# One integer step of a top-k selection, and the low parts of some matmul weights, moved from VectorE to GpSimd

## The chip, the cores and the metric

The kernel runs on one core of one Trainium2 chip. The metric is the device time of one execution in microseconds (us). The engines are named as in the profile: PE is TensorE's matmuls, PEld its weight loads, DVE is VectorE, ACT is ScalarE, POOL is GpSimd, SP is SyncE, whose queue issues most DMAs. Each engine runs its own queue in order; an instruction that waits for another engine holds back all that stand behind it.

## What is computed

Two layers of a decoder trunk on 1024 tokens of width 1024, fp32 throughout. Each layer is one wide projection, a sparse attention (branch A), a gated delta rule (branch B) and an output projection:

```
for layer in range(DEPTH):                      # 2
    h = rms_norm(x, norm_gain[layer])
    (q_a, k_a, v_a, z_a, q_i, k_i, w_i, qkv_b, z_b, beta_l, a_l, gate_l) = split(h @ w_in[layer])
    y_a = dsa_attention(rope(q_a), rope(k_a), v_a, rope(q_i), rope(rms_norm(k_i)), w_i) * silu(z_a)
    y_b = rms_norm(gated_delta_rule(silu(conv(qkv_b)), ...)) * silu(z_b)
    x = x + (sigmoid(gA) * y_a + sigmoid(gB) * y_b) @ w_out[layer]

# in dsa_attention, for each block of 128 queries
iscore = einsum('bqhs,bqh->bqs', relu(einsum('bqhd,bsd->bqhs', qib, k_idx)), wb)
iscore = where(causal, iscore, -inf)
_, sel = lax.top_k(iscore, 256)                 # each query attends to its 256 best keys
```

The change touches how the 256 best keys are found and how the weights of the first gates (`sigmoid(gA) * silu(z_a)`) are prepared.

## The kernel before, in words

A matmul in full fp32 is made of three in a rounded format: the operand is split into a high part and the rest (`split`, L152 to L156). ACT writes the high part by a cast (`w_hi`, L155), DVE subtracts it from the raw weight (`w_lo`, L156). A product is then hi·hi, hi·lo and lo·hi. `w_tiles` holds three raw tiles (`w_raw`, loaded by SP's queue) and eight of each part, so a raw tile is free for the next load when both parts are made.

In each layer `token_phase` (L411) runs the projections for q, k and v of branch A in three chunks of eight token blocks. For each block ACT copies the result to a `stage` tile (L426), POOL turns it by the rotary tables (`rope`, L270 to L275, two-input operations) and POOL's queue stores it (`qs` L432, `ks` L434, `vs` L435). After them come four gates of branch A (`gate_a`, `GATES[0]` = 4): each projects two pairs of weight tiles over two halves of the tokens. ACT takes a tanh of each result (`th`, L700) and frees its PSUM bank (tags `acc` and `wide` in turn); DVE joins it (`gate<-th,acc` and `gate<-th,gate`, L701), where the first of the two still reads the bank `acc`.

Beside the projections runs the selection (`self.beside`, taken a little further by `tick` after some matmuls). For the six blocks of 128 queries that have more than 256 keys it finds the 256th largest score of each query by bisecting the bits of its float, from bit 30 down to bit 0. There are two groups, `([5], [4, 3, 2])` and `([7], [6])`, interleaved: in each group DVE counts the keys above the threshold for the first list (L603) and ACT for the second (`t_sign`, L621, a sign with accumulation). A half-step then forms on DVE the candidate for the next bit (`cand`, L625), compares the counts (`dec`, L627) and sets the bits (`bits`, L628). The signs of the group's next half-step wait for these bits. Behind the 31 steps a tail on DVE (L632 to L686) corrects the thresholds and breaks ties with a scan per block (L675 to L685); ACT makes the signs (L665) in two buffers `t_sign`, so the sign of a block waits for the maximum (L682) of the block two before it.

`feature_phase` follows (branch B, tags `more` and `acc`): its first matmuls are those of `kf`. Its two tiles `xp` are cleared at four columns by DVE (L725). They lie where the `stage` tiles lay, so this memset waits until the last `ks` store has read its `stage`. The bank `more` is one that a gate's `wide` used.

A scheduler sets the order in each engine's queue: the program is laid out by priorities (`high_priority`, `issue_after`), and what it takes for an operation's cost moves the rows that follow.

Of the kernel before, what the change touches and what calls it, by code (L numbers as in the profile page):

```python
# [25 lines left out]
F32 = mybir.dt.float32  # L26
# [3 lines left out]
I32 = mybir.dt.int32  # L30
AF = mybir.ActivationFunctionType
OP = mybir.AluOpType
# [4 lines left out]
P = 128  # L37
# [64 lines left out]
class Trunk:  # L102
# [47 lines left out]
            nc.vector.scalar_tensor_tensor(y, t, 1.5, y, op0=OP.add, op1=OP.mult)  # L150
        return y

    def split(self, hi, lo, src):

        self.nc.scalar.copy(hi, src)  # L155
        self.nc.vector.tensor_sub(lo, src, hi.bitcast(F32))  # L156


    def identity(self):
# [6 lines left out]
    def constants(self, first):  # L166
        nc, c = self.nc, self.const
        self.ones = c.tile([P, P], F32, name="ones")
        nc.gpsimd.memset(self.ones, 1.0)

        def tri(name, fill_in, fill_out, cm, step, base, dtype=F32):
            m = c.tile([P, P], dtype, name=name)
            nc.gpsimd.memset(m, fill_in)
            nc.gpsimd.affine_select(m, m, pattern=[[step, P]], compare_op=OP.is_ge, fill=fill_out, base=base,
                                    channel_multiplier=cm)
            return m


        self.tri_in = tri("tri_in", 1.0, 0.0, -1, 1, 0)
        self.tri_out = tri("tri_out", 1.0, 0.0, 1, -1, -1)  # L180
        self.tri_mid = c.tile([P, P], F32, name="tri_mid")
        nc.vector.tensor_copy(self.tri_mid[64:], self.tri_in[64:])
        nc.vector.tensor_scalar(self.tri_mid[:64], self.tri_out[:64], -1.0, None, op0=OP.mult)
        self.causal_sel = tri("causal_sel", BIG, -BIG, 1, -1, 0)
        self.causal01 = c.tile([P, 2 * P], BF16, name="causal01")
        nc.gpsimd.memset(self.causal01, 0.0)
        nc.gpsimd.affine_select(self.causal01[:, P:], self.causal01[:, P:], pattern=[[-1, P]],
                                compare_op=OP.is_ge, fill=MASKED, base=0, channel_multiplier=1)

        self.xinit = c.tile([P, 8, 32], F32, name="xinit")  # L190
        nc.gpsimd.memset(self.xinit, 0.0)
        for q in range(4):
            nc.gpsimd.affine_select(self.xinit[32 * q:32 * q + 32], self.xinit[32 * q:32 * q + 32],
                                    pattern=[[4, 8], [-1, 32]], compare_op=OP.not_equal, fill=1.0, base=q,
                                    channel_multiplier=0)
        self.rope_tables()

        self.feat, self.ig, self.nexpa, self.dtb = [], [], [], []
        for l in range(self.depth):
            rows = first.tile([P, P], F32, name="rows", bufs=2)  # L200
            nc.sync.dma_start(out=rows[0:96], in_=self.conv_w[l].rearrange("j (t c) -> (j t) c", c=P))
            nc.sync.dma_start(out=rows[96:97], in_=self.gdn_gain[l][None, :])
            pt = self.tr()
            nc.tensor.transpose(pt[:, :97], rows[:97], self.ident[:97, :97])
            f = c.tile([P, 97], F32, name=f"feat{l}")
            nc.vector.tensor_copy(f, pt[:, :97])
            nc.vector.tensor_scalar(f[:, 96:97], f[:, 96:97], 0.25, None, op0=OP.mult)
            self.feat.append(f)
            g = c.tile([P, IDXD], F32, name=f"ig{l}")
            nc.sync.dma_start(out=g, in_=ap(self.idx_gain[l], 0, [[0, P], [1, IDXD]]))  # L210
            self.ig.append(g)
            al = c.tile([P, 8], F32, name=f"al{l}")
            nc.sync.dma_start(out=al, in_=ap(self.a_log[l], 0, [[0, P], [1, 8]]))
            nc.scalar.activation(al, al, AF.Exp)
            nc.vector.tensor_scalar(al, al, -1.0, None, op0=OP.mult)
            self.nexpa.append(al)
            db = c.tile([P, 8], F32, name=f"db{l}")
            nc.sync.dma_start(out=db, in_=ap(self.dt_bias[l], 0, [[0, P], [1, 8]]))
            self.dtb.append(db)
# [113 lines left out]
    def w_tiles(self, srcs, n):  # L333

        nc, pool = self.nc, self.wp
        raw = pool.tile([P, 512], F32, name="w_raw", bufs=3)
        for o, w, a in srcs:
            dst = raw[:, o:o + w]
            if len(a.shape) == 3:
                dst = dst.rearrange("p (k c) -> p k c", k=a.shape[1])  # L340
            nc.sync.dma_start(out=dst, in_=a)
        hi = pool.tile([P, 512], F32R, name="w_hi", bufs=KT)
        lo = pool.tile([P, 512], F32R, name="w_lo", bufs=KT)
        self.split(hi[:, :n], lo[:, :n], raw[:, :n])
        return hi, lo

    def token_weights(self, w, pieces, now=True):
# [64 lines left out]
    def token_phase(self, l, ip, ht, first):  # L412
        nc, tc = self.nc, self.tc
# [7 lines left out]
        raw = ip.tile([P, T, IDXW], F32, name="idx_raw")  # L421
        copy = lambda t, a, o: nc.scalar.copy(raw[:, t, o:o + 300], a)

        def evac(t, a, chunk):
            st = ip.tile([P, 512], F32, name="stage", bufs=3)
            nc.scalar.copy(st, a)  # L426
            rows = slice(t * P, (t + 1) * P)
            heads = 4 if chunk < 2 else 2
            v = st[:, :heads * P].rearrange("p (o h d) -> p o h d", o=1, d=P)
            self.rope(ip, v, slice(t, t + 1), self.rope_a, heads, nc.gpsimd)  # L430
            if chunk < 2:
                nc.gpsimd.dma_start(out=self.qs[rows, chunk * 512:chunk * 512 + 512], in_=st)  # L432
            else:
                nc.gpsimd.dma_start(out=self.ks[rows], in_=st[:, :256])  # L434
                nc.gpsimd.dma_start(out=self.vs[rows], in_=st[:, 256:])  # L435
# [11 lines left out]
        with tc.tile_pool(name="sel", bufs=1) as p, self.banks(wide=(2, 2)), ExitStack() as scoring:  # L447
            ps = scoring.enter_context(tc.tile_pool(name="tok", bufs=1))
            scores = {t: p.tile([P, (t + 1) * P], F32, name=f"scores{t}") for t in SEL}
            select = interleave([self.select(p, i, scores, *st) for i, st in enumerate(SEL_STAGES)])  # L450
            self.beside = itertools.chain(self.index_scores(l, ps, raw, scores), closing(scoring), select)

            for ch in range(3):
                self.proj_tokens(qkv[ch], ht, lambda t, a: evac(t, a, ch), then=qkv[ch + 1] if ch < 2 else None)
            for f in range(GATES[0]):
                self.gate_a(l, ht, f, itertools.cycle(("acc", "wide")))
            for _ in self.beside or ():
                pass
            self.beside = None
# [125 lines left out]
    def select(self, p, which, scores, on_dve, on_act):  # L585
# [6 lines left out]
        nc = self.nc  # L592
        blocks, n_dve = on_dve + on_act, len(on_dve)
        nb = len(blocks)
        sc = [scores[t] for t in blocks]
        mk = lambda n, dt=F32: p.tile([P, 4], dt, name=f"{n}{which}")[:, :nb]
        cnt, tau, dec = mk("t_cnt"), mk("t_tau"), mk("t_dec", I32)
        bits, cand, neg, neg1 = mk("t_bits", I32), mk("t_cand", I32), mk("t_neg", I32), mk("t_neg1", I32)
        f = lambda a, i: a[:, i:i + 1].bitcast(F32)

        def count(i, thr, op):
# [4 lines left out]
        for i in range(nb):  # L606
            count(i, 0.0, OP.is_ge)
            n = sc[i].shape[1]
            nc.vector.memset(tau[:, i:i + 1], float(n - TOPK if i < n_dve else n - 2 * TOPK))
        nc.vector.tensor_scalar(neg, cnt, float(TOPK), None, op0=OP.is_lt)  # L610
        nc.vector.tensor_scalar(neg1, neg, 2.0, 1.0, op0=OP.mult, op1=OP.add)
        nc.vector.tensor_scalar(bits, neg, 31, None, op0=OP.logical_shift_left)
        nc.vector.tensor_scalar(bits, bits, 1 << 30, None, op0=OP.bitwise_or)  # L613
        yield SEL_COST


        for b in range(30, -1, -1):
            for i in range(n_dve, nb):
                n = sc[i].shape[1]
                junk = p.tile([P, S], F16, name="t_sign", bufs=2)  # L620
                nc.scalar.activation(junk[:, :n], sc[i], AF.Sign, bias=f(bits, i), scale=-1.0,  # L621
                                     accum_out=cnt[:, i:i + 1])
            for i in range(n_dve):
                count(i, f(bits, i), OP.is_lt)
            nc.vector.scalar_tensor_tensor(cand, neg1 if b else neg, max(b - 1, 0), bits, op0=OP.logical_shift_left,  # L625
                                           op1=OP.bitwise_xor)
            nc.vector.tensor_tensor(dec, cnt, tau, op=OP.is_gt)  # L627
            nc.vector.scalar_tensor_tensor(bits, dec, b, cand, op0=OP.logical_shift_left, op1=OP.bitwise_xor)  # L628
            yield SEL_COST

        lo, far = mk("t_lo", I32), mk("t_far", I32)
# [36 lines left out]
        for i, t in enumerate(blocks):  # L668
            n = (t + 1) * P
# [536 lines left out]

    def run(self):
        nc, tc = self.nc, self.tc
        src = self.x.rearrange("b s d -> (b s) d")
        rest = None  # L1210
        for l in range(self.depth):
# [93 lines left out]
```

## Time and profile before

| | us |
|---|---|
| median of three runs (2589.47 to 2591.08) | 2590.01 |
| the profiled execution | 2589.74 |
| its span | 2588.0 |
| what lies around the span | 1.74 |
| PE busy | 2530.8 |
| DVE busy | 1879.1 |
| ACT busy | 1335.6 |
| POOL busy | 169.1 |

The stretch that the change touches is that of the gates and the selection's end: about 253 to 357 us in the first layer and 1528 to 1631 us in the second. PE is the engine on which the work of the program stands in a row; a gap before one of its matmuls is time that the other engines cost.

### The profile page before, as it was taken

The page shows a single profiled execution, that of the slowest core. Times are in us where ns is not written, and L with a number is a line of the kernel's source. Part 1 is how long each engine was busy: PE and PEld are TensorE (multiplying, and loading weights), DVE is VectorE, ACT ScalarE, POOL GpSimd, SP SyncE. Part 2 cuts the span into 40 slices and gives each one's busy share as a digit, 9 for nine tenths or more (in the row PEclk, how much of TensorE's full clock was granted, in tenths as well). Part 3 has the DMA queues.
Part 4 walks back from the last instruction along what each step waited for, and adds up shares of the span by engine and source line. Part 5 has one row for each costly group of instructions (what it writes and reads, how often), then busy time and mean ns, then how long its engine had stood idle before and what let it go on. Part 6 is the DMA issues. An engine that isn't in the chain of part 4 may idle for free. (4 is left out here: it accounts for less than half of the span.)

```text
span 2588.0 us, 41984 instructions
## 1 busy us (share of the span) xinstructions
PE 2530.8 (98%) x14858; PEld 2096.6 (81%) x14858; DVE 1879.1 (73%) x5092; ACT 1335.6 (52%) x3067; POOL 169.1 (7%) x438
## 2 busy tenths in 40 slices
PE   7999999999999999999999999999999999999998
PEld 7777787888888888898897777778888888878986
DVE  7569997777787763787465789777777787637876
ACT  5449944344444432787244597344444444338862
POOL 0234000000000000000002330000000000000000
PEclk9999999999999999999999999999999999999999
DMA  4122243223333331431421223333223323323314
GB/s 127 53 68 85 71 111 76 70 53 70 68 73 70 76 93 55 151 93 42 160 68 50 78 66 89 82 77 74 59 63 74 68 69 74 101 82 125 93 47 166
DMA packets 295415, 211.35 MB, mean 82 GB/s; under 512 B 72290, under 2 KB 252356, under 8 KB 295204
## 3 DMA queue, kind: packets, MB, share of 16 engines
q1 hardware_dynamic: 288388, 186.57, 26.8%
q0 software_dynamic: 6816, 22.09, 3.4%
q8 instruction: 117, 1.92, 0.3%
q14 instruction: 94, 0.77, 0.1%
HBM read 162.19 MB, written 46.40 MB: 81 GB/s over the span
## 5 line engine op out<-in xcount | busy, mean ns | idle before, releaser
L400 PE MATMUL acc<-hi_t,w_hi 128*128 128x512 f32 x1112 | 453.0, 407 | 3.3 <-ACT w_hi L155 3.1
L400 PE MATMUL acc<-hi_t,w_lo 128*128 128x512 f32 x1112 | 449.0, 404 | 3.5 <-DVE w_lo L156 3.5
L400 PE MATMUL acc<-lo_t,w_hi 128*128 128x512 f32 x1112 | 451.8, 406 | 0.0
L155 ACT CAST w_hi<-w_raw 128x512 fp32r<-128x512 f32 (+1 forms) x336 | 200.1, 603 | 269.6 <-PE acc L400 129.1
L156 DVE TENSOR_TENSOR w_lo<-w_raw,w_hi 128x512 fp32r<-128x512 f32 (+1 forms) x336 | 223.0, 670 | 137.5 <-ACT w_hi L155 118.4
L376 PE MATMUL acc<-w_hi,hi_t 128*128 128x512 f32 (+1 forms) x768 | 287.4, 375 | 5.4 <-ACT stage L426 2.8
L376 PE MATMUL acc<-w_lo,hi_t 128*128 128x512 f32 (+1 forms) x768 | 283.3, 369 | 2.6 <-DVE w_lo L156 2.5
L376 PE MATMUL acc<-w_hi,lo_t 128*128 128x512 f32 (+1 forms) x768 | 282.5, 368 | 0.0
L400 PEld LDWEIGHTS acc<-hi_t,w_lo 128*128 128x128 f32 x1112 | 209.5, 188 | 47.3 <-DVE w_lo L156 6.1
L400 PEld LDWEIGHTS acc<-hi_t,w_hi 128*128 128x128 f32 x1112 | 209.4, 188 | 46.9 <-ACT w_hi L155 5.8
L400 PEld LDWEIGHTS acc<-lo_t,w_hi 128*128 128x128 f32 x1112 | 209.5, 188 | 39.1
L400 PE MATMUL more<-hi_t,w_hi 128*128 128x512 f32 x488 | 200.2, 410 | 5.2 <-ACT th L700 5.2
L621 ACT ACTIVATE t_sign<-scores,t_bits 128x640 f16<-128x640 f32 x248 | 195.9, 794 | 16.2 <-DVE t_bits L613 13.3
L400 PE MATMUL more<-lo_t,w_hi 128*128 128x512 f32 x488 | 199.7, 409 | 0.0
L400 PE MATMUL more<-hi_t,w_lo 128*128 128x512 f32 x488 | 198.2, 406 | 0.0
L376 PEld LDWEIGHTS acc<-w_hi,hi_t 128*128 128x128 f32 x768 | 145.0, 189 | 38.3 <-issue 7.6
L376 PEld LDWEIGHTS acc<-w_lo,hi_t 128*128 128x128 f32 x768 | 145.3, 189 | 26.1 <-DVE w_lo L156 4.8
L376 PEld LDWEIGHTS acc<-w_hi,lo_t 128*128 128x128 f32 x768 | 145.2, 189 | 23.5 <-issue 1.0
L603 DVE TENSOR_SCALAR_CACHE_REDUCE t_junk<-scores,t_bits 128x768 f16<-128x768 f32 x124 | 142.1, 1146 | 4.2
L577 DVE SCALAR_TENSOR_TENSOR scores<-relu,w_idx,scores 128x384 f32<-128x384 f32 (+5 forms) x84 | 81.0, 965 | 65.0 <-ACT relu L570 60.4
L997 DVE TENSOR_TENSOR xtmp<-wide,xc 128x60 f32<-128x60 f32 (+24 forms) x496 | 105.9, 213 | 14.2
L999 DVE TENSOR_TENSOR xc<-xc,xtmp 128x60 f32<-128x60 f32 (+24 forms) x496 | 104.2, 210 | 14.0
(360 smaller groups left out, 5556.2 us busy)
## 6 DMA issues: line engine op xcount, KB each, us to landing
w_raw<-in_w_in_dram SPq DMA_DIRECT2D x272, 256.0 KB
qs<-stage POOLq DMA_DIRECT2D x32, 256.0 KB, 2.4
ya_gate<-gate SPq DMA_DIRECT2D x32, 256.0 KB
H<-rows SPq DMA_DIRECT2D x16, 512.0 KB
wide<-hscr SPq DMA_DIRECT2D x64, 128.0 KB
yb<-gate SPq DMA_DIRECT2D x32, 256.0 KB
w_raw<-in_w_out_dram SPq DMA_DIRECT2D x32, 256.0 KB
qraw<-qs SPq DMA_DIRECT2D x32, 256.0 KB
```

The costliest lines, as they stand in the source:

```text
L155: self.nc.scalar.copy(hi, src)
L156: self.nc.vector.tensor_sub(lo, src, hi.bitcast(F32))
L376: mm = nc.tensor.matmul(acc[t][:, :n], a[:, k, ts], ws[k][b][:, :n], start=k == 0 and i == 0, stop=k == KT - 1 and i == 2)
L400: mm = self.nc.tensor.matmul(acc, ws[k // 4][a][:, cs], act[b][:, k, hs], start=k == 0 and i == 0, stop=k == KT - 1 and i == 2)
L577: nc.vector.scalar_tensor_tensor(sc[:, :n], rel[half][:, :n], wc, sc[:, :n], op0=OP.mult, op1=OP.add)
L603: nc.vector.tensor_scalar(junk[:, :sc[i].shape[1]], sc[i], thr, 0.0, op0=op, op1=OP.add, accum_out=cnt[:, i:i + 1])
L621: nc.scalar.activation(junk[:, :n], sc[i], AF.Sign, bias=f(bits, i), scale=-1.0, accum_out=cnt[:, i:i + 1])
L997: nc.vector.tensor_mul(tmp[:, :n, j + 1:], ln[:, None, j, j + 1:].to_broadcast(shape), X[:, :n, j:j + 1].to_broadcast(shape))
L999: nc.vector.tensor_add(X[:, :n, j + 1:], X[:, :n, j + 1:], tmp[:, :n, j + 1:])
```

## The change

The candidate of each half-step, the exclusive-or of the bits with a shifted pattern, becomes an integer addition on POOL: `bits + steps[30 - b]`, where `steps` holds the power of two with its sign for each bit. A constant table `places` is filled once by 30 memsets on POOL, and each group makes its `steps` on DVE ahead of the loop (two small operations and one of 128 x 120 or 128 x 60). That moves 62 `cand` in each layer from DVE to POOL. During the four gates of `token_phase` the subtraction that gives `w_lo` is issued on POOL: 16 tiles of 128 x 512 in each layer. All else is the same program, laid out anew by the scheduler.

```diff
-    def split(self, hi, lo, src):
+    def split(self, hi, lo, src, eng=None):
         self.nc.scalar.copy(hi, src)
-        self.nc.vector.tensor_sub(lo, src, hi.bitcast(F32))
+        (eng or self.nc.vector).tensor_sub(lo, src, hi.bitcast(F32))
...
+        self.places = c.tile([P, 30], I32, name="places")
+        for b in range(30):
+            nc.gpsimd.memset(self.places[:, b:b + 1], 1 << (29 - b))
         self.rope_tables()
...
-        self.split(hi[:, :n], lo[:, :n], raw[:, :n])
+        self.split(hi[:, :n], lo[:, :n], raw[:, :n], self.low)
...
+            self.low = nc.gpsimd
             for f in range(GATES[0]):
                 self.gate_a(l, ht, f, itertools.cycle(("acc", "wide")))
+            self.low = None
...
-        nc.vector.tensor_scalar(neg1, neg, 2.0, 1.0, op0=OP.mult, op1=OP.add)
         nc.vector.tensor_scalar(bits, neg, 31, None, op0=OP.logical_shift_left)
         nc.vector.tensor_scalar(bits, bits, 1 << 30, None, op0=OP.bitwise_or)
+        steps = p.tile([P, 31, nb], I32, name=f"t_steps{which}")
+        sgn = mk("t_sgn", I32)
+        nc.vector.tensor_scalar(sgn, neg, -2.0, 1.0, op0=OP.mult, op1=OP.add)
+        nc.vector.tensor_tensor(steps[:, :30], self.places[:, :, None].to_broadcast([P, 30, nb]),
+                                sgn[:, None, :].to_broadcast([P, 30, nb]), op=OP.mult)
+        nc.vector.tensor_scalar(steps[:, 30], neg, -1.0, None, op0=OP.mult)
...
-            nc.vector.scalar_tensor_tensor(cand, neg1 if b else neg, max(b - 1, 0), bits, op0=OP.logical_shift_left,
-                                           op1=OP.bitwise_xor)
+            nc.gpsimd.tensor_tensor(cand, bits, steps[:, 30 - b], op=OP.add)
             nc.vector.tensor_tensor(dec, cnt, tau, op=OP.is_gt)
             nc.vector.scalar_tensor_tensor(bits, dec, b, cand, op0=OP.logical_shift_left, op1=OP.bitwise_xor)
...
+        self.low = None
```

The lines move down by up to 14: L625 is L639 after, L434 is L438, L435 is L439, L701 is L714, L680 is L693, L665 is L678, L700 is L713.

POOL's queue at the first of the four gates of the first layer, around the last `ks` store. Before:

```order
L270 TENSOR_TENSOR rope_a<-stage,sin 128x32
L271 TENSOR_TENSOR rope_b<-stage,sin 128x32
L435 DMA vs<-stage 128x256
L272 TENSOR_TENSOR stage<-stage,cos 128x2x16
L273 TENSOR_TENSOR stage<-stage,cos 128x2x16
L274 TENSOR_TENSOR stage<-stage,rope_a 128x2x16
L275 TENSOR_TENSOR stage<-stage,rope_b 128x2x16
L434 DMA ks<-stage 128x256
```

`rope` has turned the last block of keys here. The same place after, where `t_cand` is the candidate of one group:

```order
L639 TENSOR_TENSOR t_cand_2184<-t_bits_2183,t_steps_2201 128x4
L156 TENSOR_TENSOR w_lo<-w_raw,w_hi 128x512
L274 TENSOR_TENSOR rope_a<-stage,sin 128x32
L275 TENSOR_TENSOR rope_b<-stage,sin 128x32
L439 DMA vs<-stage 128x256
L276 TENSOR_TENSOR stage<-stage,cos 128x2x16
L277 TENSOR_TENSOR stage<-stage,cos 128x2x16
L156 TENSOR_TENSOR w_lo<-w_raw,w_hi 128x512
L278 TENSOR_TENSOR stage<-stage,rope_a 128x2x16
L279 TENSOR_TENSOR stage<-stage,rope_b 128x2x16
L156 TENSOR_TENSOR w_lo<-w_raw,w_hi 128x512
L438 DMA ks<-stage 128x256
```

Three `w_lo` now stand ahead of the last `ks` store in POOL's queue.

ACT's queue at the end of the second layer's selection (`t_sign` of 512 and of 384 columns are the signs of the last two blocks). Before:

```order
L665 ACTIVATE t_sign,t_cnt_16155<-scores_15085,t_bits_16158 128x512
L155 CAST w_hi<-w_raw 128x512
L700 ACTIVATE th<-acc 128x512
L665 ACTIVATE t_sign,t_cnt_16155<-scores_15084,t_bits_16158 128x384
L155 CAST w_hi<-w_raw 128x512 x2
L700 ACTIVATE th<-wide 128x512
L806 COPY xp_17916<-more 128x512
```

The same place after:

```order
L678 ACTIVATE t_sign,t_cnt_16192<-scores_15122,t_bits_16195 128x512
L155 CAST w_hi<-w_raw 128x512
L678 ACTIVATE t_sign,t_cnt_16192<-scores_15121,t_bits_16195 128x384
L713 ACTIVATE th<-acc 128x512
L155 CAST w_hi<-w_raw 128x512 x3
L713 ACTIVATE th<-wide 128x512
L819 COPY xp_17959<-more 128x512
```

A `th<-acc` and a third `w_hi` have moved between the last sign and `th<-wide`; in the first layer the `th<-acc` has moved behind that sign too.

DVE's queue at the end of the first layer's selection, from the maximum of the block of 896 columns. Before:

```order
L682 TENSOR_TENSOR t_junk<-t_junk,t_sign 128x896
L675 TENSOR_SCALAR t_eq,t_eqs_3726<-t_sign 128x512
L685 TENSOR_SCALAR scores_1082<-t_junk 128x896
L677 TENSOR_TENSOR t_less_3727<-t_cnt_2149,t_eqs_3726 128x1
L701 SCALAR_TENSOR_TENSOR gate<-th,acc 128x512
L678 TENSOR_SCALAR t_less_3727<-t_less_3727 128x1
L156 TENSOR_TENSOR w_lo<-w_raw,w_hi 128x512
L680 SCALAR_TENSOR_TENSOR t_junk<-t_eq,t_less_3727 128x512
```

The same place after:

```order
L695 TENSOR_TENSOR t_junk<-t_junk,t_sign 128x896
L688 TENSOR_SCALAR t_eq,t_eqs_3763<-t_sign 128x512
L698 TENSOR_SCALAR scores_1113<-t_junk 128x896
L690 TENSOR_TENSOR t_less_3764<-t_cnt_2180,t_eqs_3763 128x1
L691 TENSOR_SCALAR t_less_3764<-t_less_3764 128x1
L693 SCALAR_TENSOR_TENSOR t_junk<-t_eq,t_less_3764 128x512
L714 SCALAR_TENSOR_TENSOR gate<-th,acc 128x512
L694 TENSOR_TENSOR t_junk<-t_junk,t_eq 128x512
```

The gate's join has moved behind the scan of 512 columns. Between the last bits and the maximum of 896, DVE's queue of the first layer holds ten `w_lo` and four joins before, five `w_lo` and four joins after.

## Rows read from the trace of the kernel before

**Rows 1.** The page's first part: busy time, share of the span, instructions.

```profile
PE 2530.8 (98%) x14858; PEld 2096.6 (81%) x14858; DVE 1879.1 (73%) x5092; ACT 1335.6 (52%) x3067; POOL 169.1 (7%) x438
```

**Rows 2.** Stretches: busy time (instructions) of each engine, granted TensorE clock, DMA share, GB/s.

```profile
280.00:300.00 20.00, 20.00 (x88) 16.10 (x87) 18.50 (x58) 18.83 (x48) 0.00 (x0) 1.00 0.29 79
1600.00:1620.00 20.00, 20.00 (x88) 16.10 (x87) 19.07 (x46) 8.58 (x16) 1.08 (x2) 1.00 0.37 98
1620.00:1640.00 20.00, 14.76 (x54) 11.47 (x53) 15.92 (x34) 5.33 (x12) 2.16 (x4) 0.83 0.52 132
```

**Rows 3.** PE's waits, second layer, 1525 to 1640: total, times, longest.

```profile
PE more L400 <- ACT th L700: 5.2, 1, 5.2
```

**Rows 4.** Timeline of DVE and ACT, one pair of half-steps each: start, duration, instruction.

```profile
269.30 1.01 DVE L603 TENSOR_SCALAR_CACHE_REDUCE t_junk<-scores,t_bits 128x768 f16<-128x768 f32 x1
...
272.36 1.01 DVE L603 TENSOR_SCALAR_CACHE_REDUCE t_junk<-scores,t_bits 128x768 f16<-128x768 f32 x1
...
285.81 1.03 ACT L621 ACTIVATE t_sign<-scores,t_bits 128x896 f16<-128x896 f32 x1
...
288.96 1.03 ACT L621 ACTIVATE t_sign<-scores,t_bits 128x896 f16<-128x896 f32 x1
```

**Rows 5.** Timeline at the first gate: POOL, ACT, DVE; in brackets the idle time before.

```profile
257.19 0.58 POOL L434 DMA_DIRECT2D ks<-stage  x1 [0.30 <-POOL stage L275]
...
258.33 0.62 ACT L155 CAST w_hi<-w_raw 128x512 fp32r<-128x512 f32 x1 [0.78 <-DMA w_raw<-in_w_in_dram]
...
260.85 0.09 DVE L725 MEMSET xp<- 128x4 f32 x2 [2.54 <-DMA ks<-stage]
260.98 0.69 DVE L156 TENSOR_TENSOR w_lo<-w_raw,w_hi 128x512 fp32r<-128x512 f32 x1
261.58 0.16 DVE L627 TENSOR_TENSOR t_dec<-t_cnt,t_tau 128x4 int32<-128x4 f32 x1
...
262.03 0.83 ACT L621 ACTIVATE t_sign<-scores,t_bits 128x640 f16<-128x640 f32 x1 [0.90 <-DVE t_bits L628]
```

**Rows 6.** Timeline of POOL: two-input operations of two sizes.

```profile
212.22 0.31 POOL L274 TENSOR_TENSOR stage<-stage,rope_a 128x64 f32<-128x64 f32 x1
...
250.23 0.24 POOL L275 TENSOR_TENSOR stage<-stage,rope_b 128x32 f32<-128x32 f32 x1
```

**Rows 7.** Timeline of DVE: small and large operations, with POOL idle and with POOL busy.

```profile
152.59 2.27 DVE L156 TENSOR_TENSOR w_lo<-w_raw,w_hi 128x512 fp32r<-128x512 f32 x3
...
211.12 1.44 DVE L625 SCALAR_TENSOR_TENSOR t_cand<-t_neg,t_bits 128x4 int32<-128x4 int32 x1
...
271.90 0.16 DVE L625 SCALAR_TENSOR_TENSOR t_cand<-t_neg,t_bits 128x2 int32<-128x2 int32 x1
```

**Rows 8.** Timeline of DVE, ACT and PE at the second layer's end of the selection.

```profile
1594.66 0.15 DVE L628 SCALAR_TENSOR_TENSOR t_bits<-t_dec,t_cand 128x2 int32<-128x2 int32 x1
...
1627.24 0.62 DVE L682 TENSOR_TENSOR t_junk<-t_junk,t_sign 128x896 f16<-128x896 f16 x1
...
1627.96 0.61 ACT L665 ACTIVATE t_sign<-scores,t_bits 128x384 f16<-128x384 f32 x1 [4.13 <-DVE t_junk L682]
...
1629.60 0.58 ACT L700 ACTIVATE th<-wide 128x512 f32<-128x512 f32 x1
...
1630.24 0.80 PE L400 MATMUL more<-hi_t,w_hi 128*128 128x512 f32 x1 [5.24 <-ACT th L700]
...
1635.10 0.55 PE L400 MATMUL more<-hi_t,w_lo 128*128 128x512 f32 x1
```

**Rows 9.** Timeline of DVE, PE and ACT at the first layer's end of the selection.

```profile
351.99 0.62 ACT L665 ACTIVATE t_sign<-scores,t_bits 128x384 f16<-128x384 f32 x1 [4.13 <-DVE t_junk L682]
...
352.79 0.68 DVE L701 SCALAR_TENSOR_TENSOR gate<-th,acc 128x512 f32<-128x512 f32 x1
...
353.53 0.50 PE L400 MATMUL acc<-hi_t,w_hi 128*128 128x512 f32 x1
...
354.06 1.28 DVE L680 TENSOR_TENSOR_SCAN t_junk<-t_eq,t_less 128x512 f16<-128x512 f16 x1
```

More of the change, by code (lines that the diff above doesn't have):

```diff
@@ L597, in select @@
         cnt, tau, dec = mk("t_cnt"), mk("t_tau"), mk("t_dec", I32)
-        bits, cand, neg, neg1 = mk("t_bits", I32), mk("t_cand", I32), mk("t_neg", I32), mk("t_neg1", I32)
+        bits, cand, neg = mk("t_bits", I32), mk("t_cand", I32), mk("t_neg", I32)
         f = lambda a, i: a[:, i:i + 1].bitcast(F32)
```

## The prediction

> **What bounds the kernel now.** I began with the page's busy times: PE works 98% of the span, POOL 7% [rows 1]. A change to DVE and POOL can move the time only where PE stands still, so I next read the stretches of the gates and PE's waits there. While the selection's loop runs, PE, DVE and ACT are all above 90% (the first row) [rows 2]. The one large gap lies at the end: 5.2 us in the second layer, in which `more` waits for the tanh that frees its bank [rows 3], and it is the only place where the granted clock is below 1.00 (0.83 over 20 us, the last row) [rows 2].
>
> I followed that gap back. The matmul at 1630.24 waits for the `th<-wide` of 1629.60; this stands in ACT's queue behind the sign of the last block, which starts at 1627.96 having waited for the maximum of the block of 896, done 1627.24 + 0.62 [rows 8]. So the selection's end is on PE's path. From the last bits (1594.66) to this maximum are 33 us, and DVE is busy 19.07 of 20 us there [rows 2]: the tail is bound by DVE. In the first layer the same maximum releases the sign at 351.99, and PE starts `kf`'s second half at 353.53, right behind the join of 352.79 (0.60 to the next instruction) that reads the bank last [rows 9]. No large gap there, but no slack either: a later join is a later PE.
>
> What sets the loop? A pair of half-steps takes ACT 288.96 − 285.81 = 3.15 us and DVE 272.36 − 269.30 = 3.06 us [rows 4], before tanhs, casts, joins and `w_lo`. ACT waits for bits at 262.03 (0.90) [rows 5]; elsewhere in the loop it has hardly a gap. The loop is bound by ACT; work that leaves DVE there is worth little.
>
> **The change, part by part.** I call S the shift of the maximum of 896 against before, per layer.
>
> *Candidates.* One costs DVE 0.07 to 0.16 us (its last row 0.16) [rows 7]; 62 per layer make 5 to 10 us of DVE, beside ACT's chain. On POOL a candidate can start as soon as the bits are there and is needed one pair later (3.15 us). The longest work ahead of it in the token phase is one block's turn and stores, some six operations of 0.3 and two issues of 0.6: 3 us. I take 0, and as bounds −1.3 (the candidate of 211.12 that took 1.44 in place of 0.16 [rows 7] no longer holds DVE) to +0.5. The memsets lie ahead of all this on an idle POOL, and the tables' operations behind the bits for which ACT waits: 0 to +0.3, taken as 0.
>
> *One `w_lo` on POOL.* The trace has none. Two-input operations of POOL take 0.24 us for 32 columns and 0.31 for 64 [rows 6], 2.2 ns a column: 0.31 + 448 × 2.2 ns = 1.3 us for 512, an estimate. On DVE it holds the queue for 0.60 (260.98 to 261.58) [rows 5]. The Trainium skill (GPSIMD Engine Reference, Performance versus the Vector engine) gives 4497 ns for an addition of 2048 fp32 on GpSimd, 1.96 times DVE; in proportion that is an estimate of 1.1 us, by which the sum below would be about 1 us smaller. No run here shows it yet.
>
> *The first gate.* Three `w_lo` and a candidate now stand ahead of the last `ks` store in POOL's queue. They add 3 × 1.3 = 3.9 us; some 1.3 of this falls into the queue's waits, since POOL idles before this block's turn and the first weights are cast before it. The store goes out 2.6 us later than 257.19. DVE's memset, which waits for its landing and already stands 2.54 us [rows 5], follows: 263.5 in place of 260.85. Behind it on DVE stand the comparison and the bits, for which ACT waits. The `w_lo` that stood between (0.60) has left DVE, so bits and signs come 2.0 us later: **+2.0** to the loop in each layer. Bounds: 0 (`w_lo` finds gaps for all of it) and +3.
>
> *The other gates.* In ACT's queue the fourth cast moves one sign ahead. It waited 0.78 for its weights at 258.33 [rows 5], and will wait longer by up to the sign's length: 0 to +1.2 over two gates. Since ACT is 2 us late by then and the load is not, I take **+0.4**. S so far: 2.4.
>
> *The tail.* Five of ten `w_lo` leave DVE there: four to POOL, one to behind the maximum. Without a conflict that is −3.0. But the trace shows one between the two engines: `cand` took 1.44 us at 211.12 and was released when POOL's six operations ended (212.22 + 0.31) [rows 6, 7]; three `w_lo` took 2.27 in place of 1.8 at 152.59 beside POOL [rows 7]. DVE's one-input counts show nothing of it. The tail opens with some twenty small operations, many of two inputs, just when POOL has three `w_lo` in a row: 3.9 us, of which DVE uses about 1.0. DVE loses 2.9 there and saves 1.8: +1.1. The fourth costs about 0.4 and saves 0.6, the fifth saves 0.6. Sum: **+0.3**, bounds −3.0 and +1.5.
> That stall is also what the Trainium skill states (SBUF — State Buffer, SBUF: two separate sides): the port pair that the two share is locked for a whole instruction of GpSimd, and the other fully blocks. By it every such meeting costs one 512-column instruction; the trace agrees at 211.12, where one small operation outlasted several of POOL's.
>
> So S = 2.0 + 0.4 + 0.3 = **+2.7** in each layer.
>
> *Behind the maximum.* In the first layer the join that frees the bank now stands behind the scan of 512 columns (1.28 [rows 9]) and its tanh behind the last sign: some 1.4 to 1.7 later than before in its place, although a `w_lo` ahead of the scan is gone; I take 1.6. PE: 2.7 + 1.6 = +4.3. In the second layer a tanh (0.50) and a third cast (0.55) stand between the sign and `th<-wide`: 2.7 + 1.05 = +3.75. Nothing of PE's order behind it changes, so it carries to the end.
>
> *The clock.* After the 5.24 us gap the twelve matmuls from 1630.24 on run at 0.44 us each (1635.10 − 1630.24 over 11) [rows 8], at 1.2 GHz, against 20/88 = 0.23 at 2.4 GHz [rows 2]: 2.3 us. The second layer pays that already. The first gets a gap of 4.3 us, for which no row says whether the clock falls: 0 or +2.3. I take 0, since only the longest gap of this trace shows it.
>
> Sum: 2589.74 + 4.3 + 3.75 = 2597.8 for the profiled execution, whose time is 0.27 below the median of the three runs: **2598 us**.
>
> **The rivals.** *A: the relief.* POOL and DVE meet rarely, the store goes out in time, the tail is 3.0 shorter: S = −2.6. The first layer's join is at −1.0, so PE gains nothing there, its next release being near; the second gains 1.5 of its gap: 2588 us. If the gap of 5.24 shrinks enough that the clock stays up, 2.3 more: 2586. For it: DVE is what bounds the tail. Against it: ACT's order now puts a tanh and a cast ahead, and rows 7 show the meetings. To gain over 5.2 us the gap would have to vanish whole with its clock loss, S below −6.
>
> *B: nothing moves in sum.* The delay at the first gate is swallowed and the tail saves what the meetings cost, S = 0: 1.6 + 1.05 = +2.65, 2592.5 us. For it: the two ends of each term straddle 0. Against it: DVE already stands 2.54 us for that store, so whatever delays the store is paid in full.
>
> *C: worse than forecast, slower.* DVE and POOL block each other on all meetings in loop and tail: a `w_lo` on POOL, three in a row, also holds the candidate behind them (3.9 us against the 3.15 of a pair), so bits are late by 0.8 at the second and third gates; with the upper ends of the tail, S is 2.7 + 1.6 + 1.2 = 5.5. PE then waits 7.1 and 6.5, and the first layer's clock falls: 2589.7 + 7.1 + 6.5 + 2.3 = 2606 us. It decides from where POOL's `w_lo` passes about 1.3 us.
>
> *D: it does not do what it says*: the integer addition is so slow that the candidate is late every half-step. With 31 pairs and 0.5 us each this is +15 and more per layer, over 2620 us. POOL's 32-column operation at 0.24 us speaks against it.
>
> **How the numbers follow.** Forecast (S from 1.3 to 4, 2595 to 2601): 0.45. B (S from −1 to 1.3, 2590 to 2595): 0.25. C: 0.15. A: 0.12, a third of it below 2584.8. D: 0.03. What can be told from no change is 0.2%, 5.2 us: 2584.8 to 2595.2. Slower takes the forecast, C and D, less a little of the forecast at its edge: 0.6. Same takes B and most of A: 0.35. Faster 0.05. Eight of ten: down to the better part of A, 2587, and up to C's sum, 2606; most of the forecast's own weight lies in 2595 to 2601.
>
> **What would show it.** In the changed kernel: `w_lo` on POOL at 1.1 to 1.4 us; the last `ks` store 2 to 3 us after 257.19 and DVE's wait before the memset at about 5 us; ACT's wait for the bits behind it near 3 us; some two-input DVE operations of over 1 us beside POOL's `w_lo` in the tail; the wait of `more` in the second layer near 9 us, and a new one of about 4 us before `kf`'s second half in the first. The forecast falls if DVE's small operations keep 0.16 us beside POOL, or if the store is issued at its old time: then A or B holds. It falls the other way if the first layer's clock goes below 1.00.

## The result, and the profile after

The changed kernel takes 2603.7 us (median, 2602.4 to 2606.7), against 2590.5 us before: 1.0053 times as long, 95% interval 1.0041 to 1.0065, or 13 us slower. The forecast was 2598 us in a range of 2587 to 2606. The profiled execution took 2602.45 us with a span of 2600.7, 12.7 more than before.

The first lines of the page after. DVE has lost 7 us of work and POOL has gained 68 (its operations take longer there); PE shows 4.6 us more for the same matmuls [rows 1]:

```profile
PE 2535.4 (97%) x14858; PEld 2101.2 (81%) x14858; DVE 1871.8 (72%) x4944; ACT 1335.0 (51%) x3067; POOL 237.3 (9%) x624
```

PE's waits after, first those of the first layer (180 to 370 us), then those of the second (1450 to 1660). Columns: total, times, longest:

```profile
PE acc L404 <- DVE gate L714: 3.6, 1, 3.6
PE acc L404 <- ACT w_hi L155: 2.3, 2, 1.2
PE acc L404 <- POOL w_lo L156: 2.0, 3, 0.9
...
PE more L404 <- ACT th L713: 8.6, 1, 8.6
PE acc L404 <- ACT w_hi L155: 4.7, 3, 2.5
PE acc L404 <- POOL w_lo L156: 2.2, 3, 1.2
```

The first line is the gap that the prediction placed ahead of `kf`'s second half. The gap of `more` has grown from 5.2 to 8.6 [rows 3]; in the second layer a cast now holds PE for 2.5 us as well. The stretches after (busy time of each engine, granted clock, DMA share, GB/s):

```profile
240.00:260.00 20.00, 18.31 (x72) 14.20 (x71) 16.32 (x38) 18.59 (x46) 13.76 (x39) 0.91 0.23 68
...
340.00:360.00 20.00, 16.42 (x66) 12.92 (x65) 19.62 (x38) 7.24 (x15) 1.99 (x4) 0.93 0.26 85
...
1560.00:1580.00 20.00, 17.79 (x64) 13.93 (x65) 14.54 (x35) 15.94 (x40) 7.02 (x12) 0.83 0.26 67
...
1640.00:1660.00 20.00, 15.59 (x61) 12.57 (x62) 13.37 (x28) 6.73 (x13) 1.62 (x3) 0.83 0.49 130
```

The clock is below 1.00 in all four; in the kernel before it is 1.00 in the same four stretches and falls only near the end of the second layer's selection (0.83) [rows 2].

**Where the 12.7 us are.** I set the starts of the same ACT instructions of both traces side by side. The shift is −0.7 at the first signs of the first selection and −0.3 at the second signs. Each trace with the candidate on POOL has this step of 0.4 in both layers, and those without it have not; the tables of steps are made there. Then it is −1.0 at the first gate, +0.4 behind the `ks` store, +1.2 at the last bits of the loop, +2.4 at the maximum of 896 and +3.9 at the join that frees the bank. Then +5.2, after six matmuls at the lower clock. It is +6.5 at the first signs of the second selection and +6.9 at the second: 1.6 of that arises at 1290 to 1320 us between the layers, where the clock fell in this execution (0.94) and not in that of before. The traces of e1, e6 to e10, e12 and e13 below show the same fall, and those of e2, e3, e5 and e11 do not; it does not go with the low parts, so I count it as no part of the change. In the second layer: +5.8 at the first gate, +8.3 behind the store, +11.2 behind the second gate, +11.5 at the last bits, +12.9 at the maximum of 896, +14.2 at `th<-wide`, and +13.1 after the matmuls at the lower clock, which are fewer than before.

**The first gate.** Timeline after of POOL, DVE and ACT, first layer, then second (start, duration, instruction, idle time before):

```profile
252.84 1.28 POOL L156 TENSOR_TENSOR w_lo<-w_raw,w_hi 128x512 fp32r<-128x512 f32 x1
255.12 1.70 DVE L640 TENSOR_TENSOR t_dec<-t_cnt,t_tau 128x2 int32<-128x2 f32 x1 [1.45 <-ACT t_sign L635]
257.17 1.27 POOL L156 TENSOR_TENSOR w_lo<-w_raw,w_hi 128x512 fp32r<-128x512 f32 x1
258.39 0.58 POOL L438 DMA_DIRECT2D ks<-stage  x1
261.98 0.06 DVE L738 MEMSET xp<- 128x4 f32 x1 [2.20 <-DMA ks<-stage]
...
1540.88 0.58 POOL L438 DMA_DIRECT2D ks<-stage  x1
1545.81 0.06 DVE L738 MEMSET xp<- 128x4 f32 x1 [3.54 <-DMA ks<-stage]
1546.29 0.83 ACT L635 ACTIVATE t_sign<-scores,t_bits 128x640 f16<-128x640 f32 x1 [2.99 <-DVE t_bits L641]
```

A `w_lo` on POOL takes 1.28 us (estimate 1.3). The store goes out at 258.39, 1.2 later than before [rows 5] although the loop ran 1.0 earlier here; DVE's memset follows it. In the second layer the memset also runs 4.9 us after the store's issue in place of 3.8, and ACT stands 3 us. The later landing is no accident of this execution: in the four traces with the first gate's low parts on POOL (this one, e2, e5, e8) this store lands 4.2 to 4.8 us after its issue, in the others at 3.1 to 3.6 (e13: 4.3). Why is not shown.

**The second gate of the second layer.** ACT, POOL and PE after:

```profile
1560.39 0.61 ACT L155 CAST w_hi<-w_raw 128x512 fp32r<-128x512 f32 x1
1561.05 0.50 PE L404 MATMUL acc<-hi_t,w_hi 128*128 128x512 f32 x1 [2.47 <-ACT w_hi L155]
1561.85 4.21 POOL L156 TENSOR_TENSOR w_lo<-w_raw,w_hi 128x512 fp32r<-128x512 f32 x3
1563.18 0.79 PE L404 MATMUL acc<-hi_t,w_lo 128*128 128x512 f32 x1 [1.16 <-POOL w_lo L156]
1563.77 0.63 PE L404 MATMUL acc<-hi_t,w_hi 128*128 128x512 f32 x1
1566.38 0.62 ACT L155 CAST w_hi<-w_raw 128x512 fp32r<-128x512 f32 x1 [1.73 <-DMA w_raw<-in_w_in_dram]
1571.18 0.60 ACT L713 ACTIVATE th<-acc 128x512 f32<-128x512 f32 x1 [2.33 <-PE acc L404]
```

The same tanh before:

```profile
1560.72 0.60 ACT L700 ACTIVATE th<-acc 128x512 f32<-128x512 f32 x1 [0.30 <-PE acc L400]
```

The casts stand between the signs of the loop. A loop that the first gate has made 2.5 us later brings the second gate's casts late, PE waits 2.5 and 1.2 us for them and their low parts, and twelve matmuls follow each other at 0.43 us in place of 0.23: 2.4 us. The raw tiles come free late, and the fourth cast waits 1.73 us for its load (0.85 before). But ACT then stands another 2.33 us at the tanh that waits for PE, so it is PE's lateness (10.5 at this tanh), and with it the lower clock, that delays the loop once more; 0.7 us come on top because this tanh now stands one sign further ahead in ACT's queue. In e3 and e8 below, where the loop is not late at this gate, PE waits for no cast there and no matmul runs at the lower clock.

**The tail.** DVE and POOL of the first layer after, then ACT and PE at the end of the second layer:

```profile
319.95 3.80 POOL L156 TENSOR_TENSOR w_lo<-w_raw,w_hi 128x512 fp32r<-128x512 f32 x3 [3.11 <-ACT w_hi L155]
319.98 1.29 DVE L652 TENSOR_SCALAR t_lo<-t_neg 128x4 int32<-128x4 int32 x1
321.18 0.16 DVE L645 TENSOR_SCALAR t_lo<-t_bits 128x2 int32<-128x2 int32 x1
321.25 1.27 DVE L647 TENSOR_SCALAR t_far<-t_bits 128x2 int32<-128x2 int32 x1
322.51 1.27 DVE L646 TENSOR_SCALAR t_lo<-t_lo 128x2 int32<-128x2 int32 x1
...
1641.13 0.61 ACT L678 ACTIVATE t_sign<-scores,t_bits 128x384 f16<-128x384 f32 x1 [5.13 <-DVE t_junk L695]
1641.74 0.58 ACT L713 ACTIVATE th<-acc 128x512 f32<-128x512 f32 x1
1642.22 1.64 ACT L155 CAST w_hi<-w_raw 128x512 fp32r<-128x512 f32 x3
1643.77 0.59 ACT L713 ACTIVATE th<-wide 128x512 f32<-128x512 f32 x1
1644.41 0.79 PE L404 MATMUL more<-hi_t,w_hi 128*128 128x512 f32 x1 [8.60 <-ACT th L713]
```

While POOL makes three `w_lo`, three DVE operations on two or four numbers a partition take 1.3 us, one for each of POOL's; between them one slips through. And the tanh that frees `more` stands 1.0 us further behind the last sign than before [rows 8].

### The profile page after: what moved, and what is told of

The parts are those of the page before. It is cut to its first block, busy times and chain, and to the rows that moved or that the text cites. A ratio compares the mean times of both kernels' runs of the same rounds, so it can differ in the third digit from the quotient of the medians.

```text
span 2600.7 us, 42161 instructions
## 1 busy us (share of the span) xinstructions
PE 2535.4 (97%) x14858; PEld 2101.2 (81%) x14858; DVE 1871.8 (72%) x4944; ACT 1335.0 (51%) x3067; POOL 237.3 (9%) x624
## 5 line engine op out<-in xcount | busy, mean ns | idle before, releaser
L404 PE MATMUL acc<-hi_t,w_hi 128*128 128x512 f32 x1112 | 454.8, 409 | 10.5 <-ACT w_hi L155 7.0
L156 DVE TENSOR_TENSOR w_lo<-w_raw,w_hi 128x512 fp32r<-128x512 f32 (+1 forms) x304 | 202.2, 670 | 140.1 <-ACT w_hi L155 120.6
L635 ACT ACTIVATE t_sign<-scores,t_bits 128x640 f16<-128x640 f32 x248 | 196.1, 798 | 18.2 <-DVE t_bits L619 13.1
L792 POOL TENSOR_SCALAR_AFFINE_SELECT H<-H 128x1024 f32<-128x1024 f32 x16 | 19.0, 1190 | 1056.3 <-DMA H<-rows 326.0
```

Of the source, the lines that this page charges most:

```text
L156: (eng or self.nc.vector).tensor_sub(lo, src, hi.bitcast(F32))
L404: mm = self.nc.tensor.matmul(acc, ws[k // 4][a][:, cs], act[b][:, k, hs], start=k == 0 and i == 0, stop=k == KT - 1 and i == 2)
```

## The experiments

My theory after the trace: the loss comes from the low parts of two of the four gates, the first (through the store and the memset that waits for it) and the fourth (through the blocking and the changed order in the tail), and not from the candidate. Rivals: the candidate's round trip; a price of every low part on POOL; the blocking at the first gate and not the store. The ratios are to runs of the kernel before on the same chip, with 95% intervals.

| run | low parts on POOL, gates 1 to 4 | other | median us | ratio |
|---|---|---|---|---|
| e1 | none | candidate on POOL | 2590.0 | 0.9993 (0.9984 to 1.0002) |
| e2 | 1 2 3 4 | candidate on DVE | 2600.6 | 1.0038 (1.0024 to 1.0051) |
| e3 | 2 3 4 | candidate on POOL | 2598.3 | 1.0028 (1.0017 to 1.0040) |
| e5 | 1 2 3 | candidate on POOL | 2597.5 | 1.0026 (1.0014 to 1.0038) |
| e6 | 2 3 | candidate on POOL | 2591.0 | 1.0000 (0.9991 to 1.0009) |
| e7 | none | before, late zeros | 2589.8 | 0.9994 (0.9986 to 1.0003) |
| e8 | 1 2 3 | candidate on POOL, late zeros | 2591.6 | 1.0002 (0.9993 to 1.0010) |
| e9 | none | candidate on POOL, late zeros | 2589.1 | 0.9994 (0.9985 to 1.0002) |
| e10 | first half of 4 | candidate on POOL | 2593.3 | 1.0013 (1.0005 to 1.0022) |
| e11 | second half of 4 | candidate on POOL | 2590.8 | 1.0004 (0.9994 to 1.0013) |
| e12 | none | before, own last sign | 2587.9 | 0.9991 (0.9982 to 1.0000) |
| e13 | none | before, own last sign, late zeros | 2584.6 | 0.9981 (0.9972 to 0.9989) |

**e1, the candidate alone.**

```diff
-            self.low = nc.gpsimd
```

> The kernel after with all low parts back on DVE: only the candidate is added on POOL. My theory (the loss comes from the low parts on POOL: the ks store queued behind them, and POOL holding up DVE at the start of the tail): no loss is left. The token stretch keeps its gain of 0.7 to 1.1 us per layer, the order behind the last maximum is that of before, and the gap ahead of more stays near 5 us: 2587 to 2591 us. Rival (the round trip of bits and candidate over two engines costs the loop): signs wait for bits in every pair and the time stays above 2597 us.

No loss, as expected; a gain is not resolved. **e2, the low parts alone** (the table of steps and POOL's addition taken out):

```diff
-            nc.gpsimd.tensor_tensor(cand, bits, steps[:, 30 - b], op=OP.add)
+            nc.vector.scalar_tensor_tensor(cand, neg1 if b else neg, max(b - 1, 0), bits, op0=OP.logical_shift_left,
+                                           op1=OP.bitwise_xor)
```

> The kernel before with only the low parts of all four gates on POOL; the candidate stays on DVE. The three low parts stand ahead of the last ks store and four in the tail, as in the changed kernel, and the order behind the last maximum is changed likewise. My theory (the low parts are the whole loss): 2601 to 2605 us, as the changed kernel or slightly above, since the candidate's gain in the token stretch is missing. Rival (the loss needs both: candidates held behind three low parts in POOL's queue): 2597 us or less.

9.8 us of loss without the candidate, just under the expected 2601 and over the rival's 2597. The low parts carry most of the loss. Whether the candidate adds the rest (13 against 10 us) stays open: the intervals of the two overlap.

**e3, e5 and e6: which gates.** The low parts of the first gate, of the fourth, of both back on DVE:

```diff
             for f in range(GATES[0]):
+                self.low = nc.gpsimd if f > 0 else None          # e3
+                self.low = nc.gpsimd if f < 3 else None          # e5
+                self.low = nc.gpsimd if f in (1, 2) else None    # e6
```

> The kernel after with the low parts of the first of the four gates on DVE, those of the other three on POOL. My theory: the last ks store goes out at its old time, the wait at the first gate falls back to that of before (about 0.9 us on ACT), the second layer loses its 2.5 us gap for a cast at the second gate, and the tail's loss stays: S near 1 us plus the changed order (1.6 and 1.0), about 2596 to 2599 us. Rival (the store costs nothing, the tail is all): the time stays at 2602 to 2605 us.

> The kernel after with the low parts of the fourth gate on DVE, those of the first three on POOL. The order behind the last maximum is then that of before, and POOL is idle in the tail. My theory: no one-microsecond small operations on DVE behind the last bits; the delay from the ks store stays (1.4 and 2.5 us, and a gap at the second layer's second gate): 2595 to 2599 us. Rival (the store is all): the time stays at 2601 us or more.

> The kernel after with the low parts of the first and the fourth gate on DVE, of the second and third on POOL. My theory (two causes, which add): both delays are gone, 2588 to 2592 us, as with the candidate alone. Rival (a low part on POOL costs wherever it stands, since it locks DVE out or holds the candidate behind three of them): 2595 us or more.

All three medians came out as the theory had them, and the rivals fell, though the interval of e5 just reaches its rival's 2601. The fourth gate's share is 7.3 us (e3 against e6), the first's is 6.5 us (e5 against e6), each known to some 4 us by the intervals; together 13.8, which fits the loss of the whole change. The eight tiles of the two gates between cost nothing that can be measured, though the trace of e6 shows single small operations of 0.8 and 1.2 us there.

**e7, e8 and e9: the store and the memset.** The zeros that DVE wrote during the first gate are written in front of their first use, from data that is there then:

```diff
-            for a in self.xps:
-                nc.vector.memset(a[:, 0:4], 0.0)
...
+        if hd["h"] == 0 and name != "vv":
+            nc.vector.tensor_scalar(xp[:, 0:4], xp[:, 4:8], 0.0, None, op0=OP.mult)
         for j in range(3):
             nc.vector.scalar_tensor_tensor(dst, xp[:, 1 + j:1 + j + S], cw(j), dst, op0=OP.mult, op1=OP.add)
```

> The kernel before, with the zeros of the two xp tiles written in front of their first use (four columns times zero) and not by a memset during the first gate, so that DVE no longer waits for the last ks store there (2.54 us in the trace of before). My theory (that wait reaches PE through bits, signs and the last block): ACT's idle 0.90 + 0.40 us of the first layer and 1.21 + 0.41 of the second are gone, the selection ends 1.3 to 1.6 us earlier; the second layer's gap of 5.24 shrinks by as much, the first layer has no gap to give back: 1.5 to 3 us faster than before. Rival (ACT's loop hides it): within 0.5 us of before.

> The run with the fourth gate's low parts on DVE and the first three gates' on POOL, with the zeros of xp written late as well. Theory M (the first gate's loss runs over the ks store and the memset that waits for it): the loss of 6 to 7 us against before goes, 2589 to 2592 us. Rival L (it is GpSimd's low parts that hold DVE's comparison and bits for 1.5 us each at the first gate, and late casts): DVE's small operations stay at 1.5 us, and the time stays 4 us or more above before.

> The candidate alone on POOL, all low parts on DVE, and the zeros of xp written late. If the gain of the candidate in the token stretch (0.6 to 1.1 us of the loop per layer) and that of the late zeros (1.3 to 1.6) add, the selection ends about 2.5 us earlier in each layer: 3 to 4 us faster than before, 2586 to 2588 us. If they do not add (ACT bound loop): as with the late zeros alone.

e8 tells the two causes at the first gate apart. POOL, DVE and ACT there:

```profile
255.42 1.72 DVE L640 TENSOR_TENSOR t_dec<-t_cnt,t_tau 128x2 int32<-128x2 f32 x1 [1.44 <-ACT t_sign L635]
257.25 1.57 DVE L641 SCALAR_TENSOR_TENSOR t_bits<-t_dec,t_cand 128x2 int32<-128x2 int32 x1
258.75 0.58 POOL L438 DMA_DIRECT2D ks<-stage  x1
261.20 0.83 ACT L635 ACTIVATE t_sign<-scores,t_bits 128x640 f16<-128x640 f32 x1
```

The store is as late as in the changed kernel and DVE is blocked as long, yet the loss of the first gate is gone (2591.6 against 2597.5): the blocking by itself is hidden there, and it is the memset behind the late store that costs. From 200 us to the end of the loop in the first layer the queues of ACT, DVE and POOL hold the same order in e5 and e8 but for the two memsets. In e7 and e9 the expected 1.5 to 4 us are not resolved: the medians are 0.5 and 1.2 us below before, with intervals that hold 1.0000. The trace of e7 says where the gain goes. The loop comes 1.3 and 1.6 us forward at the first gate of the two layers, and then meets a tanh that waits for PE, which is no earlier. ACT in e7:

```profile
265.38 0.60 ACT L700 ACTIVATE th<-wide 128x512 f32<-128x512 f32 x1 [1.05 <-PE wide L400]
...
276.11 0.60 ACT L700 ACTIVATE th<-wide 128x512 f32<-128x512 f32 x1 [0.33 <-PE wide L400]
```

1.4 us of the wait that I took away come back as these, and 0.3 to 0.6 us of it is left at the end of the loop.

**e10 and e11: blocking or order in the tail.** Two of the fourth gate's four low parts on POOL, the rest of the gates' on DVE. The tiles are counted through the four gates (`n_low`):

```diff
+LOW = (12, 13)    # e10; e11: (14, 15)
...
+        if self.n_low is not None:
+            eng = nc.gpsimd if self.n_low in LOW else None
+            self.n_low += 1
```

> Candidate on POOL, low parts on DVE but for the first two of the fourth gate's four, which are on POOL at the start of the tail. The order behind the last maximum is that of before, so this holds the blocking alone. Theory (blocking and order share the tail's loss): DVE's small operations of the tail that meet the two take 1.2 us each; two low parts off DVE repay 1.2 us of it: 0 to +1.5 us against the candidate alone, 2590 to 2592 us. Rival (the blocking is all of the tail's loss, the order costs nothing): half of the 7 us, 2593 us or more.

> Candidate on POOL, low parts on DVE but for the last two of the fourth gate's four, which are on POOL; as many as in the run with the first two. With these two the scheduler puts the join behind the scan of 512 columns and a tanh and a third cast ahead of the tanh that frees more, as in the changed kernel. Theory (blocking and order each cost): the time of the first two's run or a little less blocking, and 1.3 to 1.6 us in the first layer and 1.0 in the second for the order, with a clock loss after the new gap: 2594 to 2598 us. Rival (the order costs nothing, PE waits for something later anyway): 2590 to 2593 us.

From the last bits to the maximum of 896, in the first and second layer, DVE takes 32.6 and 32.6 us before, 33.8 and 34.0 after, 34.1 and 34.1 in e10, 31.7 and 31.9 in e11; in e1, without low parts on POOL, 32.6 and 33.5. POOL and DVE in e10, then in e11; the last line is PE in e11:

```profile
317.86 2.56 POOL L158 TENSOR_TENSOR w_lo<-w_raw,w_hi 128x512 fp32r<-128x512 f32 x2 [3.07 <-ACT w_hi L157]
317.92 1.27 DVE L658 TENSOR_SCALAR t_lo<-t_neg 128x4 int32<-128x4 int32 x1
319.17 1.27 DVE L653 TENSOR_SCALAR t_far<-t_bits 128x2 int32<-128x2 int32 x1
...
318.45 1.30 POOL L158 TENSOR_TENSOR w_lo<-w_raw,w_hi 128x512 fp32r<-128x512 f32 x1 [4.12 <-ACT w_hi L157]
318.50 1.27 DVE L662 TENSOR_TENSOR t_step<-t_far,t_bits 128x4 int32<-128x4 int32 x1
322.04 1.28 POOL L158 TENSOR_TENSOR w_lo<-w_raw,w_hi 128x512 fp32r<-128x512 f32 x1 [2.29 <-ACT w_hi L157]
322.32 1.03 DVE L658 TENSOR_SCALAR t_lo<-t_neg 128x2 int32<-128x2 int32 x1
...
352.87 0.50 PE L410 MATMUL acc<-hi_t,w_hi 128*128 128x512 f32 x1 [0.77 <-DVE gate L720]
```

With the order of before (but for one `w_lo` that now follows the scan of 512), two low parts on POOL at the head of the tail lengthen it by 1.5 us in the first layer. In the second it is 1.5 against before but 0.7 against e1, in whose trace a `w_lo` on DVE waits 0.8 us. The kernel takes 3.4 us longer: my 2590 to 2592 was too low, and the 2593.3 is where the rival began. In e11, with the changed order, each of the two meets fewer small operations and the tail is 0.7 to 0.8 shorter, but the time is no better than that of before: PE waits 0.8 for the join in the first layer, and 5.5 for `more` in the second. My 2594 to 2598 missed. So the blocking is shown to cost; the order's price is seen in e11's trace alone (a gap of 0.8 us although the maximum comes 2.2 us earlier than before), and its share in the 7.3 us isn't settled.

**e12 and e13: the last sign.** In the kernel before, the last block's sign gets a buffer of its own, and so a place ahead of the casts and tanhs that stood behind it:

```diff
+            if n == 384:
+                sg[i] = p.tile([P, n], F16, name="t_last", bufs=1)
+            else:
+                sg[i] = p.tile([P, S], F16, name="t_sign", bufs=2)[:, :n]
```

> The kernel before, with a sign buffer of its own for the last block (384 columns), so that its sign stands early in ACT's queue and nothing that waits for the maximum of 896 stands ahead of the tanh that frees more. My theory (the second layer's gap of 5.24 us and the clock loss of 2.3 us behind it come from that one place in ACT's queue): the gap falls to 1 us or less and the clock stays up, 5 to 7 us faster than before, about 2584 us. Rival (another part of the selection's end holds PE as long, a join or a bank): the gap moves to the next place and the time changes by under 2 us.

> The kernel before with the last block's own sign buffer and with the zeros of xp written late. If the selection's end still holds PE in either layer the two add: 0.5 to 1.5 us below the run with the buffer alone. If PE no longer waits for the selection, they do not add: within 0.5 us of it.

e12 falls between the two, and its interval reaches 1.0000: the sign is gone, and a cast that waits for its load is next. ACT in the second layer of e12, then PE's waits at 1600 to 1640 of e12 and of e13:

```profile
1629.00 0.62 ACT L155 CAST w_hi<-w_raw 128x512 fp32r<-128x512 f32 x1 [2.60 <-DMA w_raw<-in_w_in_dram]
1629.53 0.59 ACT L704 ACTIVATE th<-wide 128x512 f32<-128x512 f32 x1
...
PE more L400 <- ACT th L704: 4.2, 1, 4.2
...
PE more L400 <- ACT th L704: 3.2, 1, 3.2
```

Its gap is still 4.2 us and the clock still falls. With the late zeros added (e13) the gap is 3.2, no matmul there runs at the lower clock, and the time is 0.19% below before (interval 0.11% to 0.28%): faster than both kernels.

## Why the prediction was right, step by step

- **What bounds the kernel**, the selection's end on PE's path in both layers: right; both gaps stand where they were placed (3.6 before `kf`'s second half, 8.6 before `more`).
- **Candidates at 0**: the tables show as 0.4 us at the start of each loop (taken as 0, with +0.3 as the bound). Then the loop gained 0.6 and 1.1 us in the token stretch, within the bounds given; but e2, e7, e12 and e13, with the candidate on DVE, gain 0 to 0.6 and 0 to 1.1 there too, so it is not shown that this gain is the candidate's. e1 bears out that tables and candidates together cost nothing that can be measured.
- **One `w_lo` at 1.3 us**: 1.28. The Trainium skill's figure (GPSIMD Engine Reference, Performance versus the Vector engine) scaled to 512 columns gave 1.1; the measurement decides, and it is a row's extrapolation that held.
- **The first gate at +2.0 per layer through the store**: +1.4 and +2.5, mean 1.9; the mechanism is shown by e8. Of the signs named for it, ACT's wait near 3 us came in the second layer alone. In the first, DVE waited 2.2 us before the memset and not about 5, since POOL had held the two operations ahead of it (1.70 and 1.54).
- **The other gates at +0.4**: +0.8 and +3.2. This is the term that was mis-sized. I moved one cast by a sign and forgot that all casts stand in the loop: a loop that is late makes PE wait for the next gate's casts, the clock falls, and the gate's tanhs then wait for a late PE and hold the loop. In the second layer that made 2.9 us at one gate. In the first, two tanhs behind the eight slow matmuls of the first gate made 0.4.
- **The tail at +0.3**: +1.2 and +1.4, near the upper bound of 1.5 and so mis-sized too; blocking was forecast and seen, though mostly on operations of one input.
- S, counted from the second signs of each selection, was 2.7 in the first layer, as forecast, and 6.0 in the second in place of 2.7. That the first layer meets the forecast is luck: its parts were −0.6, +1.4, +0.8 and +1.2 where 0, +2.0, +0.4 and +0.3 stood.
- **Behind the maximum, +1.6 and +1.05**: the join came 1.5 later than the maximum's shift (3.9 against 2.4), `th<-wide` 1.3 (14.2 against 12.9).
- **The clock at 0**: the second mis-sized term, taken from the wrong row. Only the longest gap of the trace before shows the fall, but a gap of 3.6 us (six matmuls at 1.2 GHz), gaps of 1.1 and 0.6 us close together (eight) and of 2.5 and 1.2 (twelve) show it after. It cost 1.2 us net in the first layer's end. The falls at the gates reached the loop, and with it the selection's end, through the tanhs that wait for PE, as told above. The gap of 8.6 was followed by fewer slow matmuls (five) than that of 5.2 before (eleven).

The sum was 8.05 us; the profiled executions differ by 12.7, of which 1.6 is the fall of the clock between the layers and 11 the change. That the time lies in the range is in part luck: it is above the forecast's own 2595 to 2601 and nearer to C's sum, which set the upper end. The sign that the prediction named for that side came, the first layer's clock below 1.00 (0.91 and 0.93). C also named the second and third gates as places of extra loss, by the candidates behind three `w_lo`; e6 and e8 show no such loss, so for the second gate its place was right and its cause wrong.

## What to carry to other kernels

Look at what else the queue of an idle engine carries before giving it work: here one 128 KB store in POOL's queue, waited for by a memset that DVE ran long before its result was needed, turned three operations of 1.3 us on an idle engine into some 6.5 us of loss over the two layers. Work that leaves a bound engine repays less than its duration if the engine that takes it blocks the first one during short serial operations. And where PE's operands are made between the steps of another loop, a delay of that loop is a delay of PE's next operands, and a PE that comes late holds the loop in turn: follow it to the next gate before calling it a shift.

## What the runs showed of the hardware

- DVE operations of one input on two or four int32 numbers a partition (a shift, a mask) were held up for the whole of POOL's two-input operation, 1.27 to 1.29 us in place of 0.17, as were those of two inputs (1.27, 1.7). Counts with an accumulator (1.28 for 1024 columns) and small memsets (0.06) ran beside POOL as always. I had expected two-input operations alone to be held.
- Between two operations of POOL that follow each other without a gap, one DVE operation got through (321.18 and the next, held, at 321.25); in e2 a set of bits was held for 3.5 us over several.
- POOL's addition of 128 x 4 int32 took 0.20 us, hardly less than its 0.24 for 32 columns of fp32.
- The granted clock between the two layers fell in some executions of like kernels and stayed up in others: 0.94 or 1.00 at 1290 to 1320 us, about 1.6 us of time. Gaps of 1.0 to 1.1 and 0.5 to 0.6 us at the first gate of the first layer were followed by eight slow matmuls in the changed kernel and in e3, and by none in e1, e8 and e10. The time of such a fall can't be read off one gap's length.
